# Low parts of 30 weight blocks kept in DRAM by the first group and loaded by the other three

## The chip, the cores and the metric

The kernel runs on one core of a Trainium2 chip. The metric is the device time of one execution in microseconds; the profile is one execution of the same program taken by the hardware profiler. TensorE (PE in the profile, with its weight loads as PEld) does the matmuls, VectorE is DVE, ScalarE is ACT, GpSimd is POOL, and SyncE (SP) issues most loads. Each engine works through its own queue in order.

## The reference

One layer of a hybrid block over 2048 positions of width 1024, in float32. The input is normalized and multiplied by one wide matrix `w_in`; its columns feed three branches:

```
h    = rms_norm(x, pre_mix_g)
proj = h @ w_in          # 1536 attention columns, 1792 recurrent columns, 2048 gate columns
y_a  = chunk_band_attention(q, k, v, rel_bias)      # chunks of 64, 8 earlier chunks
y_b  = rwkv7_time_mix(p_rwkv, ...)                  # a scan over the 2048 positions
merged = sigmoid(p_gate_a) * (y_a @ proj_a) + sigmoid(p_gate_b) * (y_b @ proj_b)
x = x + rms_norm(merged @ w_out)
x = x + rms_norm(relu(rms_norm(x) @ w_up)**2 @ w_down)
```

The recurrent branch mixes each column with that of the position before, derives decays and rates from it with two small matrices, and updates a 64 x 64 state per head.

## The kernel before, in words

The sequence is worked through in four groups of 512 positions. For each group there are three stages in turn: the recurrent stage (`phase_rwkv`), the attention stage (`phase_attention`) and the merge (`phase_merge`), which also normalizes the next group's input. After the four groups come the two matrices of the last line of the layer, which work on two halves of 1024 positions.

A matmul in float32 is done as three matmuls in a faster type: each operand is split into a high part, a rounded copy, and a low part, what the rounding left. The product is high x high, high x low and low x high. `wsplit` (L70) does this for a block of weights: SyncE loads the raw block of 128 x 1024 numbers (512 KB) into one of two `wraw` tiles (`load_raw`, L64), ScalarE casts it into one of two `whi` tiles (L81), and VectorE subtracts the cast from the raw block into one of two `wlo` tiles (L83). A tile is reused as soon as all that read it are through.

`dense(col)` (L118) is the product of one such block, 128 columns of `w_in`, with the group's normalized input `hh`, `hl`. It is 24 matmuls on one bank `psd`: an octet with `whi` and `hh`, an octet with `whi` and `hl`, and last an octet with `wlo` and `hh` (in the profile `hh,wlo`; the names after the arrow are sorted). So the low part is needed in the last third of a block. A recurrent stage has 30 such blocks: 14 of the recurrent columns, by `mix` (L393), and 16 of the gates, by `gate` (L786). The attention stage has 12 more. The weights are the same in every group, and each group loads and splits them anew. In the first group the first two blocks are loaded ahead, and their low parts are made by GpSimd.

`mix` takes the bank out with ScalarE into `pr` and into `out`; GpSimd copies the last column of the group before (`carry`, L399 and L400) in front of `pr`, and VectorE adds the two (L402). `rwkv_pre` and `rwkv_trans` prepare matrices for each chunk of 64 positions with many small matmuls and VectorE operations (`n2t`, `AR`, `BK`, `TQ`), `rwkv_inverse` runs 31 steps of two VectorE operations (L621, L627), and `rwkv_chunk` (L738 to L743) goes through the chunks one after the other: two matmuls on TensorE, then `ST` on VectorE, which the next chunk needs. `rwkv_post` normalizes the result; its `yn` (L761) waits for a root that GpSimd takes (L759).

The order of each engine's queue is set by a planner: it simulates the whole program with a cost for every instruction and appends to each queue whatever is ready first, earlier program text first among those that are ready. A transfer's place in SyncE's queue is planned in the same way. A few places are fixed by hand: `queue_behind` puts one instruction behind another in its queue without a wait, `follow` (L112) does so for the cast and the subtraction of a block, behind the instructions that emptied the bank three blocks before, and `place` with the numbers at the head of the file (`BLOCKS`, `TURNED`, `FIFTH`, `BONUS`, `SCORES`, `TURNS`) puts the first matmuls of the small chains behind a given matmul of the blocks of the stage, counted from its start.

Of the kernel before, what the change touches and what calls it, by code (L numbers as in the profile page):

```python
# [9 lines left out]
F32 = mybir.dt.float32  # L10
BF16 = mybir.dt.bfloat16
F32R = mybir.dt.float32r
# [4 lines left out]
DRAM = bass.MemoryType.DRAM  # L17

P = 128
D = 1024  # L20
KB = D // P
# [17 lines left out]
BONUS = {(0, 1): 138, (1, 0): 258}  # L39
SCORES = 150  # L40
TURNS = {1: (588, 592)}
DEC = math.exp(-0.5)

ATT0 = 0
# [12 lines left out]
class Block:  # L57
# [54 lines left out]
    def follow(self):  # L112

        for ins, done in zip((self.high.ins, self.low), self.emptied[-3] if len(self.emptied) > 2 else ()):
            if done is not None:
                self.queue_behind(ins, done.ins)

    def dense(self, col):  # L118

        first = bool(self.raws)  # L120
        wh, wl = self.wsplit(self.w_in(col), "w", KB, P, lower=self.nc.gpsimd if first else None)
        if first:
            n = 1 - len(self.raws)
            self.queue_behind(self.high.ins, self.highs[n])
        self.follow()
        ps = self.pd.tile([P, G], F32, tag="d", name="psd")
        terms = [(wh[:, k], wl[:, k], self.h[0][:, k], self.h[1][:, k]) for k in range(KB)]
        if first:
            pairs = [(u, h) for u, _, h, _ in terms] + [(v, h) for _, v, h, _ in terms] + [(u, l) for u, _, _, l in terms]
            self.mm = [  # L130
                self.nc.tensor.matmul(ps, l, r, start=n == 0, stop=n == len(pairs) - 1).ins
                for n, (l, r) in enumerate(pairs)
            ]
            self.queue_behind(self.mm[0], self.last_transpose)
        else:
            self.mm = self.mm3(ps, terms, True)
        self.dl += self.mm
        return ps
# [19 lines left out]
    def constants(self, ctx, mixing):  # L158
        tc, nc, a = self.tc, self.nc, self.a
        keep = ctx.enter_context(tc.tile_pool(name="const", bufs=1))  # L160
        cp = mixing.enter_context(tc.tile_pool(name="mconst", bufs=1, side="right"))
        dp = ctx.enter_context(tc.tile_pool(name="scratch", bufs=1, space=DRAM))
        nrow = sum(n for _, n in ROWS)
        self.cst = cp.tile([P, nrow], F32, name="cst")
        nc.sync.dma_start(self.cst, a["cst"])
# [279 lines left out]
    def rwkv_pre(self, g, p, rp, NA, between=lambda: None):  # L445
# [20 lines left out]
        between()  # L466
        nc.vector.tensor_scalar(tw, tw, -0.5 * DEC, -0.5 * DEC, ALU.mult, ALU.add)
        cum = tw
# [279 lines left out]
    def rwkv_post(self, p, R):  # L748
# [18 lines left out]
        for h in range(2):  # L767
            ps = self.pr.tile([C, 4, P], F32, tag="wus", name="ps_yt")
            for j in range(4):
                mm = nc.tensor.transpose(ps[:, j], yn[:, h * 4 + j], self.ident)  # L770
                if j == 0 and p in TURNS:
                    self.place(mm, TURNS[p][h])
            cs = slice(h * 4, h * 4 + 4)
# [876 lines left out]
```

## Time and profile before

| | us |
|---|---|
| median of 3 runs (lowest, highest) | 3199.82 (3198.31, 3202.85) |
| the profiled execution | 3198.07 |
| its span, first to last instruction | 3196.4 |
| TensorE busy in the span | 3147.3 |
| VectorE busy in the span | 2235.8 |
| ScalarE busy | 1578.7 |
| GpSimd busy | 613.8 |

Where the groups begin and end in the span:

| group | recurrent stage | attention stage and merge |
|---|---|---|
| 0 | 14.2 to 282.2 | 282.2 to 482.8 |
| 1 | 482.8 to 746.0 | 746.0 to 976.0 |
| 2 | 976.0 to 1239.0 | 1239.0 to 1468.6 |
| 3 | 1468.6 to 1731.6 | 1731.6 to about 1990 |

How to read the rows: a group of instructions is given by its line in the kernel, its engine, its operation and the tiles it writes and reads (out<-in), with its shape and count; then come its busy time, the mean duration of one in ns, the engine's idle time just before these instructions and what ended it. A row of a stretch of time gives the busy time and the number of instructions of each engine, the granted clock of TensorE, the busy share of the DMA rings and GB/s. Matmuls of a run overlap: eight in a row, each of 389 ns, take 1.98 us. A row of waits names the waiting instruction, whom it waited for, and the sum, the number and the longest of the waits. A row that starts with two numbers has the start in us from the begin of the span and the duration.

### The profile page before, as it was taken

The page shows a single profiled execution, that of the slowest core. Times are in us where ns is not written, and L with a number is a line of the kernel's source. Part 1 is how long each engine was busy: PE and PEld are TensorE (multiplying, and loading weights), DVE is VectorE, ACT ScalarE, POOL GpSimd, SP SyncE. Part 2 cuts the span into 40 slices and gives each one's busy share as a digit, 9 for nine tenths or more (in the row PEclk, how much of TensorE's full clock was granted, in tenths as well). Part 3 has the DMA queues.
Part 4 walks back from the last instruction along what each step waited for, and adds up shares of the span by engine and source line. Part 5 has one row for each costly group of instructions (what it writes and reads, how often), then busy time and mean ns, then how long its engine had stood idle before and what let it go on. Part 6 is the DMA issues. An engine that isn't in the chain of part 4 may idle for free. (4 is left out here: it accounts for less than half of the span.)

```text
span 3196.4 us, 49803 instructions
## 1 busy us (share of the span) xinstructions
PE 3147.3 (98%) x18800; PEld 2575.3 (81%) x18800; DVE 2235.8 (70%) x3668; ACT 1578.7 (49%) x2511; POOL 613.8 (19%) x1119
## 2 busy tenths in 40 slices
PE   8999999999999999999999999999999999999998
PEld 6877788778888877888877888888888878888887
DVE  6785667776767786767876776877656768765564
ACT  5435645445745445745534755454544454444343
POOL 3222012132112222112222101221211112210000
PEclk9999999999999999999999999999999999999999
DMA  6245473157573246574236466554877866547565
GB/s 192 86 135 189 134 259 129 60 172 244 175 260 129 77 141 245 186 235 160 94 116 228 160 208 261 192 179 162 293 268 251 281 225 213 170 156 244 191 221 174
DMA packets 197477, 598.82 MB, mean 187 GB/s; under 512 B 25570, under 2 KB 25708, under 8 KB 197236
## 3 DMA queue, kind: packets, MB, share of 16 engines
q1 hardware_dynamic: 139124, 415.24, 40.1%
q0 software_dynamic: 48896, 163.61, 13.6%
q10 hardware_dynamic: 9216, 16.78, 1.4%
q8 instruction: 148, 2.42, 0.3%
q14 instruction: 93, 0.76, 0.1%
HBM read 431.67 MB, written 167.01 MB: 187 GB/s over the span
## 5 line engine op out<-in xcount | busy, mean ns | idle before, releaser
L1469 PE MATMUL ps_dn<-fop 128*128 128x512 f32 x2688 | 610.8, 389 | 0.0
L1469 PEld LDWEIGHTS ps_dn<-fop 128*128 128x128 f32 x2688 | 504.1, 188 | 104.7 <-DVE fop L83 0.2
L81 ACT CAST whi<-wraw 128x1024 fp32r<-128x1024 f32 x232 | 243.5, 1049 | 284.4 <-PE psd L92 202.5
L83 DVE TENSOR_TENSOR wlo<-wraw,whi 128x1024 fp32r<-128x1024 f32 x230 | 280.6, 1220 | 125.4 <-ACT whi L81 80.2
L92 PE MATMUL psd<-hh,whi 128*128 128x512 f32 x1328 | 357.9, 398 | 1.1 <-ACT k L401 1.0
L92 PE MATMUL psd<-hh,wlo 128*128 128x512 f32 x1328 | 356.8, 398 | 0.0
L92 PE MATMUL psd<-hl,whi 128*128 128x512 f32 x1328 | 354.3, 397 | 0.0
L92 PEld LDWEIGHTS psd<-hl,whi 128*128 128x128 f32 x1328 | 243.6, 188 | 47.9
L92 PEld LDWEIGHTS psd<-hh,wlo 128*128 128x128 f32 x1328 | 242.7, 188 | 48.3
L92 PEld LDWEIGHTS psd<-hh,whi 128*128 128x128 f32 x1328 | 241.2, 188 | 50.0 <-ACT k L401 1.6
L83 DVE TENSOR_TENSOR fop<-xraw,fop 128x1024 fp32r<-128x1024 f32 x112 | 137.0, 1223 | 176.2 <-ACT fop L81 175.8
L81 ACT CAST fop<-xraw 128x1024 fp32r<-128x1024 f32 x112 | 117.8, 1052 | 251.0 <-PE ps_dn L1469 191.9
L1339 POOL DMA_DIRECT2D xd<-X x192 | 104.1, 542 | 380.3 <-ACT X L1336 318.2
L83 DVE TENSOR_TENSOR fop<-wdraw,fop 128x1024 fp32r<-128x1024 f32 x112 | 136.6, 1219 | 19.7 <-ACT fop L81 19.4
L81 ACT CAST fop<-wdraw 128x1024 fp32r<-128x1024 f32 x112 | 117.6, 1050 | 35.7 <-DMA wdraw<-in_w_down_dram 22.7
L994 DVE CUSTOM_DVE_ANT_0 sc<-bias,ps_s 128x640 f32<-128x640 f32 (+4 forms) x128 | 93.8, 733 | 39.3 <-PE ps_s L988 23.3
L1012 DVE TENSOR_TENSOR PTl<-ps_pt,PTh 128x640 fp32r<-128x640 f32 (+4 forms) x128 | 94.3, 737 | 27.7 <-ACT PTh L1011 26.8
L1001 ACT ACTIVATE sc<-sc,mn 128x640 f32<-128x640 f32 (+4 forms) x128 | 97.8, 764 | 31.8 <-DVE mn L994 30.4
L81 ACT CAST s12h<-s 128x1024 fp32r<-128x1024 f32 x32 | 33.7, 1053 | 155.5 <-PE ps_u L92 155.5
L92 PE MATMUL ps_p<-yh,whi 128*128 128x512 f32 x256 | 101.7, 400 | 4.9 <-DVE th L1149 2.2
L92 PE MATMUL ps_p<-yl,whi 128*128 128x512 f32 x256 | 101.5, 397 | 0.3 <-DVE yl L83 0.2
L1178 PE MATMUL ps_o<-whi,mh 128*128 128x512 f32 x256 | 100.5, 392 | 0.7 <-DVE o L1189 0.6
(374 smaller groups left out, 6804.0 us busy)
## 6 DMA issues: line engine op xcount, KB each, us to landing
wraw<-in_w_in_dram SPq DMA_DIRECT2D x168, 512.0 KB, 3.7
xraw<-xd SPq DMA_DIRECT2D x112, 512.0 KB, 4.5
xd<-X POOLq DMA_DIRECT2D x192, 256.0 KB, 4.7
wraw<-in_w_up_dram SPq DMA_DIRECT2D x80, 512.0 KB, 4.4
wdraw<-wd SPq DMA_DIRECT2D x64, 512.0 KB, 4.8
wdraw<-in_w_down_dram SPq DMA_DIRECT2D x48, 512.0 KB, 5.0
gd<-gate ACTq DMA_DIRECT2D x64, 256.0 KB, 2.5
wd<-cmb POOLq DMA_DIRECT2D x64, 256.0 KB, 3.7
```

Of the source, the lines that this page charges most:

```text
L81: high = self.high = self.nc.scalar.copy(hi, src)
L83: self.low = lower.tensor_tensor(lo, src, hi.bitcast(F32), ALU.subtract).ins
L92: mm.append(nc.tensor.matmul(ps, l, r, start=n == 0, stop=n == last).ins)
L994: least = nc.vector.tensor_tensor_reduce(sc[:, 0:n], bias[:, s0:640], pss[:, c0 : c0 + n], 1.0, 3.0e38, ALU.add, ALU.min, mn,)
L1001: nc.scalar.activation(sc[:, 0:n], sc[:, 0:n], AF.Exp, scale=-1.0, bias=mn, accum_out=sm[:, col : col + 1])
L1012: nc.vector.tensor_tensor(lv, pst[:, 0:nk], hv.bitcast(F32), ALU.subtract)
L1178: nc.tensor.matmul(ps[t], l[:, k, ts], r[:, k % 2], start=k == 0 and j == 0, stop=k == KB - 1 and j == 2)
L1339: nc.gpsimd.dma_start(self.xd[q][i // 2][:, i % 2], src)
L1469: nc.tensor.matmul(ps, o[:, l, k, sl], o[:, r, k], start=start and n == 0, stop=stop and n == end)
```

## The change

`LOWS` names the blocks 12 to 41 of `w_in` by their number, which are the 14 recurrent blocks and the 16 gate blocks. When a group comes to such a block for the first time, it splits it as before and GpSimd then issues a store of the low part into a DRAM tile of its own. When a later group comes to it, the raw block is loaded and cast as before, and SyncE issues a load of the kept low part into the `wlo` tile; VectorE's subtraction is gone there. `follow` passes over the low part that it no longer has. The 12 attention blocks stay as they were.

```diff
 TURNS = {1: (588, 592)}
+LOWS = range(12, 42)
...
         for ins, done in zip((self.high.ins, self.low), self.emptied[-3] if len(self.emptied) > 2 else ()):
-            if done is not None:
+            if done is not None and ins is not None:
                 self.queue_behind(ins, done.ins)
 
     def dense(self, col):
 
         first = bool(self.raws)
-        wh, wl = self.wsplit(self.w_in(col), "w", KB, P, lower=self.nc.gpsimd if first else None)
+        kept = self.lows.get(col)
+        if kept is None:
+            wh, wl = self.wsplit(self.w_in(col), "w", KB, P, lower=self.nc.gpsimd if first else None)
+            if col in self.keep_lows:
+                kept = self.lows[col] = self.dp.tile([P, KB, P], F32, name=f"wlow{col // P}")
+                self.nc.gpsimd.dma_start(kept, wl.bitcast(F32))
+        else:
+            raw = self.load_raw(self.w_in(col), KB, P)
+            wh, wl = (self.wp.tile([P, KB, P], F32R, tag="w" + x, bufs=2, name="w" + n) for x, n in (("h", "hi"), ("l", "lo")))
+            self.high = self.nc.scalar.copy(wh, raw)
+            self.low = None
+            self.nc.sync.dma_start(wl.bitcast(F32), kept)
         if first:
...
-        dp = ctx.enter_context(tc.tile_pool(name="scratch", bufs=1, space=DRAM))
+        dp = self.dp = ctx.enter_context(tc.tile_pool(name="scratch", bufs=1, space=DRAM))
+        self.lows = {}
+        self.keep_lows = {i * P for i in LOWS}
```

## The prediction, made before the changed kernel ran

> **What bounds the kernel now.** I read the page's busy line first, then its groups, then each recurrent stage with the busy times by stage, then who ended TensorE's waits there, and last the order of time around the longest wait.
>
> ```profile
> span 3196.4 us, 49803 instructions
> ```
> ```profile
> PE 3147.3 (98%) x18800; PEld 2575.3 (81%) x18800; DVE 2235.8 (70%) x3668; ACT 1578.7 (49%) x2511; POOL 613.8 (19%) x1119
> ```
> ```profile
> L1469 PE MATMUL ps_dn<-fop 128*128 128x512 f32 x2688 | 610.8, 389 | 0.0
> ```
> ```profile
> L83 DVE TENSOR_TENSOR wlo<-wraw,whi 128x1024 fp32r<-128x1024 f32 x230 | 280.6, 1220 | 125.4 <-ACT whi L81 80.2
> ```
>
> TensorE is busy 98% of the span. The last row is the work that the change takes away in part: VectorE's subtraction for one 512 KB weight block, 1.22 us, 230 times. The four rows below are the recurrent stages of groups 0 to 3, each from the first `psd` matmul to the first of the attention.
>
> ```profile
> core 0: us, PE busy (x) PEld busy (x) DVE busy (x) ACT busy (x) POOL busy (x), PEclk, DMA share, GB/s
> 14.20:282.20 268.00, 263.73 (x2188) 210.92 (x2189) 201.40 (x413) 122.93 (x208) 72.29 (x117) 1.00 0.44 141
> 482.80:746.00 263.20, 259.79 (x2190) 209.26 (x2189) 193.49 (x399) 118.83 (x203) 71.58 (x124) 1.00 0.41 132
> 976.00:1239.00 263.00, 259.79 (x2190) 209.24 (x2189) 193.50 (x399) 118.82 (x203) 71.65 (x124) 1.00 0.40 132
> 1468.60:1731.60 263.00, 259.80 (x2190) 209.24 (x2189) 193.51 (x399) 118.83 (x203) 71.65 (x124) 1.00 0.40 132
> ```
>
> In the stages that lose the subtractions TensorE idles 3.4, 3.2 and 3.2 us, 9.8 us together. VectorE is busy 193.5 of 263 us there (74%), so it is loaded but not the bound. The clock is 1.00 throughout. Who ended TensorE's waits in the third of these stages:
>
> ```profile
> engine line waited for: us in total, times, longest us
> PE ps_st L738 <- DVE ST L743: 1.1, 1, 1.1
> PE ps_s L723 <- DVE TQ L716: 0.4, 1, 0.4
> PE ps_g L92 <- DVE yn L761: 0.4, 1, 0.4
> PE psd L92 <- ACT k L401: 0.3, 1, 0.3
> ```
>
> None of them is for a low part. VectorE ends 1.9 us of waiting in a stage, and 1.1 of it is one step of the recurrence.
>
> **The change part by part.**
>
> *Subtractions removed, groups 1 to 3.* 90 x 1.22 = 110 us of VectorE's time go, 36.6 us in a stage. What that is worth is what it does to the three waits on VectorE. For the 1.1 us one, VectorE in order of time:
>
> ```profile
> 1134.35 1.22 DVE L83 TENSOR_TENSOR wlo<-wraw,whi 128x1024 fp32r<-128x1024 f32 x1
> ```
> ```profile
> 1136.53 0.73 DVE L514 SCALAR_TENSOR_TENSOR AR<-k,nkk,E 64x512 f32<-64x512 f32 x1
> 1137.84 0.17 DVE L489 TENSOR_SCALAR n2t<-ps_ss 128x8 f32<-128x8 f32 x1 [0.58 <-PE ps_ss L487]
> 1138.04 0.75 DVE L514 SCALAR_TENSOR_TENSOR AR<-k,nkk,E 64x512 f32<-64x512 f32 x1
> ```
> ```profile
> 1145.05 0.75 DVE L533 SCALAR_TENSOR_TENSOR r<-r,cst,tk 128x512 f32<-128x512 f32 x1
> 1145.71 0.47 DVE L743 SCALAR_TENSOR_TENSOR ST<-ps_st,gC,S 128x64 f32<-128x64 f32 x2
> ```
>
> From 1137.84 VectorE works without a break until the awaited `ST`. The subtraction at 1134.35 lies ahead of the `n2t` operation, which waits for TensorE anyway; with the order kept, taking 1.22 us away only lengthens that 0.58 us wait, and the gain is 0. If the planner uses the room to put the second `AR` (0.75 us) ahead of `n2t`, the `ST` comes 0.75 us sooner, and somewhat more if another one moves up. I take 0.8 us: the planner places by readiness, and all the inputs of `AR` are there. The other two waits:
>
> ```profile
> 1204.07 0.69 DVE L1231 TENSOR_TENSOR cmb<-cmb 128x512 f32<-128x512 f32 x1 [7.58 <-DMA cmb<-in_w_down_dram]
> ```
> ```profile
> 1237.38 0.69 DVE L761 TENSOR_TENSOR yn<-ps_y,grs 128x512 f32<-128x512 f32 x1 [2.07 <-POOL grs L759]
> ```
>
> Ahead of `TQ` VectorE had idled 7.58 us for a DMA, and ahead of `yn` it idled 2.07 us for GpSimd. A lighter VectorE does nothing for either: 0. Sum 3 x 0.8 = -2.4 us; bounds 0 and all the idle time, -9.8 us. What is late next in these places is the same `TQ`, `yn` and the PSUM release by `k`.
>
> *Low parts loaded, groups 1 to 3.* 90 loads of 512 KB are added on SP's queue. A load's tile is free when TensorE has used the low part of the block before the last, and TensorE uses the low part in the last third of a block. So the room is from the end of one `hh,wlo` octet to the start of the next but one. At a stage's start, with the DMA rings full in between, and at the tightest place:
>
> ```profile
> 979.58 1.98 PE L92 MATMUL psd<-hh,wlo 128*128 128x512 f32 x8
> ```
> ```profile
> 990.97 1.98 PE L92 MATMUL psd<-hh,wlo 128*128 128x512 f32 x8
> ```
> ```profile
> 1159.68 1.98 PE L92 MATMUL psd<-hh,wlo 128*128 128x512 f32 x8
> ```
> ```profile
> 1170.56 1.98 PE L92 MATMUL psd<-hh,wlo 128*128 128x512 f32 x8
> ```
> ```profile
> 980.00:985.00 5.00, 5.00 (x23) 4.13 (x22) 2.01 (x3) 3.28 (x6) 1.90 (x6) 1.00 1.01 337
> ```
>
> Room 990.97 - 981.56 = 9.4 us and 1170.56 - 1161.66 = 8.9 us. The same-sized weight loads of the stage, by their line:
>
> ```profile
> L67 SPq DMA_DIRECT2D wraw<-in_w_in_dram x30: 327/328/333, 979.1 to 1234.8; - x30
> ```
> ```profile
> DMA to landing us min/median/max: 3.4/3.7/7.6
> ```
>
> Issue 0.33 and landing 3.7: 4.0 us in the median, 7.9 at worst, against 8.9: hidden. In the full window a further 0.52 MB at 337 GB/s adds 1.6 us: 9.5 against 9.4, so 0.1 us at one place in a stage; I take 0. The stage's DMA share rises from 0.40: the 30 raw loads are 15.7 of its 34.7 MB (132 GB/s x 263 us), so 30 more make about 0.40 x 50.4/34.7 = 0.58, below full. On SP's queue a raw load can now stand behind a low load that waits for TensorE. The raw load stood behind VectorE's subtraction before, since that read the raw tile last; now ScalarE's cast alone frees it. Behind a low load it starts at latest at the end of block n-2 and lands 4 to 8 us later, with two blocks (six octets, 1170.56 - 1159.68 = 10.9 us, 1.81 us each) until its block begins: hidden. Attention's `KK` and `VV` loads follow the last low load in the same way.
>
> *Low parts stored, group 0.* 30 DMAs on GpSimd's queue, each after the subtraction. The nearest rows are the 512 KB store of `kc` and the carry copies that could queue behind a store (in the stage 14.2 to 282.2):
>
> ```profile
> L960 POOL DMA_DIRECT2D kc<-KK x12: 682/724/736, 297.9 to 1355.2; - x12
> ```
> ```profile
> DMA to landing us min/median/max: 3.1/3.8/6.7
> ```
> ```profile
> L399 POOL COPY pr<-carry 128x1 f32<-128x1 f32 x13 | 9.5, 729 | 32.1 <-DVE k L402 15.5 <-DVE r L402 9.1 <-DVE X L627 3.5
> ```
> ```profile
> L400 POOL COPY carry<-pr 128x1 f32<-128x1 f32 x14 | 5.3, 379 | 35.4 <-ACT pr L398 35.3
> ```
>
> 30 x 0.72 = 21.7 us on an engine that is busy 72.3 of 268 us. GpSimd idles 67.5 us ahead of those copies alone, so most stores lie in idle time; a store caught in front of a copy costs at most 0.72 us, passed on to VectorE's `out` and the release of `pr`. Bounds 0 and +21.7; I take +0.5, near the end at which GpSimd's idle time lies. The store also holds the low tile until it has landed: 0.72 + 3.8 = 4.5 us (7.4 at worst) after a subtraction. The closest pair of subtractions into one tile is
>
> ```profile
> 100.78 1.18 DVE L83 TENSOR_TENSOR wlo<-wraw,whi 128x1024 fp32r<-128x1024 f32 x1
> ```
> ```profile
> 108.40 1.22 DVE L83 TENSOR_TENSOR wlo<-wraw,whi 128x1024 fp32r<-128x1024 f32 x1
> ```
>
> 6.4 us apart: hidden in the median, 1.0 us late at worst.
>
> *TensorE's order.* The planner orders each engine by simulated costs, so a new order follows from other costs. In the trace it shows as broken runs: an undisturbed matmul of this shape takes 389 ns, the `psd` ones more on average in the third stage:
>
> ```profile
> L92 PE MATMUL psd<-hh,wlo 128*128 128x512 f32 x240 | 63.9, 397 | 0.0
> ```
>
> (397 - 389) x 720 = 5.8 us in a stage is what the breaks cost. Half as many or half again as many make 2.9 us a stage, 8.6 over three, either way; nothing says which: 0.
>
> *Sum.* The profiled execution took 3198.07 us for a span of 3196.4. 3198.07 - 2.4 + 0.5 = 3196.2. The median of the runs shown is 3199.82, 1.75 above the profiled one, so in its terms 3197.9.
>
> [...]
>
> **The rivals.**
>
> *A, faster.* VectorE's release carries further: the chains reach TensorE earlier, all idle time goes from three stages, 3199.8 - 9.8 = 3190.0; with half of the breaks gone as well, 3181. For: VectorE at 74% and in-order. Against: only 1.9 of some 3.2 us wait for VectorE, and 0.8 of that for other causes. Chance 0.19; the weight-load rule above adds 0.01.
>
> *B, slower: the low load lands late.* It decides where issue and landing exceed 8.9 us. If a low load must let a raw load of 3.7 us pass first in a full window, it lands after 0.33 + 7.6 + 3.7 = 11.6 us: 2.2 us late at the 9.4 us room, 2.7 at 8.9. With four such places in a stage (three at its start, one at 1160) 4 x 2.3 x 3 = +28: 3227. Against: median landing 3.7, rings at 0.40. Chance 0.08.
>
> *C, slower: a worse order.* Half again as many breaks in three stages: 3199.8 + 8.6 = 3208.4. For: the places of the chains in TensorE's order are numbers written for the old costs. Against: those numbers bind the costliest chains either way. Chance 0.12.
>
> *D, slower: GpSimd's stores.* Every store stands in front of a copy that VectorE waits for: +21.7, 3221.5. The idle time above speaks against it: 0.02. [...]
>
> **How the numbers follow.** A difference under 0.2% (6.4 us) can't be told from none here. My forecast and all small sums lie inside it: 0.58. Faster by more is A, 0.20; slower by more is B, C and D, 0.22. The likeliest time is 3197.9. The range reaches from 3189, past A's idle time, to 3209, past C; left out are A with the breaks (0.07), B and D.
>
> **What would show it.** Right: 140 `wlo<-wraw` subtractions instead of 230, VectorE near 157 us in stages 1 to 3, TensorE's busy time there unchanged at 259.8 and its idle time at 2.4 to 3.2 us; no wait of TensorE for a low load; a DMA share near 0.58. Wrong: TensorE waiting for `wlo` (B), a `psd` mean well off 397 ns (A or C), more than 4.3 us of idle in stage 0 or VectorE waiting for a carry copy (D).

## The result, and the profile after

| | before | after |
|---|---|---|
| median (lowest, highest) of 4 runs each, us | 3199.07 (3196.69, 3202.85) | 3216.47 (3210.49, 3219.30) |
| ratio, 95% interval | | 1.0051 (1.0033 to 1.0068) |
| profiled execution, its span, us | 3198.07, 3196.4 | 3219.30, 3217.3 |

The change makes the kernel slower, by 17.4 us in the median. The profiled execution of the changed kernel is the slowest of its four. Line numbers of the changed kernel are 1 to 14 higher: the cast in a group that loads its low parts is L131, the copies of the inverse XT (L637 before) and Z (L655) are L651 and L669, a gate's emptying of its bank (L790) is L804.

The page's head, and the groups of the subtraction and of the new loads (KB each, median us to landing):

```profile
span 3217.3 us, 49953 instructions
...
PE 3155.4 (98%) x18800; PEld 2581.4 (80%) x18800; DVE 2136.9 (66%) x3578; ACT 1578.3 (49%) x2511; POOL 606.9 (19%) x1149
...
L84 DVE TENSOR_TENSOR wlo<-wraw,whi 128x1024 fp32r<-128x1024 f32 x140 | 170.9, 1221 | 90.3 <-ACT whi L82 60.9
...
wlo<-wlow SPq DMA_DIRECT2D x90, 512.0 KB, 4.6
```

The 90 subtractions are gone and VectorE is 99 us lighter. TensorE issues the same 18800 matmuls, is busy 8.1 us longer (3155.4 against 3147.3) and idle 12.8 us longer (61.9 against 49.1). The four recurrent stages, each from its first `psd` matmul to the first of the attention:

```profile
core 0: us, PE busy (x) PEld busy (x) DVE busy (x) ACT busy (x) POOL busy (x), PEclk, DMA share, GB/s
14.00:284.90 270.90, 265.69 (x2188) 212.88 (x2189) 201.74 (x413) 122.69 (x208) 89.68 (x147) 0.99 0.60 197
486.30:753.50 267.20, 261.77 (x2189) 210.26 (x2188) 161.63 (x370) 119.11 (x203) 63.69 (x124) 0.99 0.54 184
983.40:1253.50 270.10, 262.00 (x2190) 210.50 (x2189) 161.67 (x370) 119.06 (x203) 63.64 (x124) 0.99 0.55 183
1482.10:1751.00 268.90, 261.97 (x2189) 210.43 (x2189) 161.73 (x370) 119.25 (x203) 63.67 (x124) 0.99 0.55 184
```

Their lengths are up by 2.9, 4.0, 7.1 and 5.9 us, 19.9 of the 20.9 us by which the span grew. All the rest of the kernel is 1.0 us longer. Who ended TensorE's waits in the third of these stages (line waited for: total, times, longest):

```profile
PE ps_t L674 <- ACT Z L669: 2.7, 2, 2.3
PE psd L93 <- ACT gate L804: 2.0, 1, 2.0
PE ps_y L756 <- DVE ST L757: 1.1, 1, 1.1
PE ps_g L93 <- DVE yn L775: 0.9, 1, 0.9
PE ps_A L599 <- DVE BR L583: 0.5, 1, 0.5
```

No wait is for a low part. The two longest are new, and both are for ScalarE, an engine that the change leaves with the same work. Its queue in order of time, before and then after, around the end of the second inverse of that stage:

```profile
1179.43 1.06 ACT L81 CAST whi<-wraw 128x1024 fp32r<-128x1024 f32 x1
...
1181.54 0.69 ACT L790 ACTIVATE gate<-psd,hgb 128x512 f32<-128x512 f32 x1
...
1184.87 1.06 ACT L81 CAST whi<-wraw 128x1024 fp32r<-128x1024 f32 x1 [2.64 <-PE psd L92]
1190.42 1.24 ACT L637 COPY XT<-XD 32x512 f32<-32x512 f32 x2 [4.49 <-DVE XD L632]
```

```profile
1192.83 1.25 ACT L651 COPY XT<-XD 32x512 f32<-32x512 f32 x2 [5.20 <-DVE XD L646]
...
1195.25 1.04 ACT L131 CAST whi<-wraw 128x1024 fp32r<-128x1024 f32 x1
1196.20 0.68 ACT L804 ACTIVATE gate<-psd,hgb 128x512 f32<-128x512 f32 x1
...
1206.03 1.04 ACT L131 CAST whi<-wraw 128x1024 fp32r<-128x1024 f32 x1 [6.78 <-DMA wraw<-in_w_in_dram]
1207.10 1.18 ACT L669 COPY Z<-ps_t 32x512 f32<-32x512 f32 x2
```

Counting the stage's blocks from 0: before, the cast of block 26 (1179.43) and the emptying of block 24's bank (1181.54) stood ahead of XT, and so did the cast of block 27 (1184.87); ScalarE then waited 4.49 us for VectorE's XD with nothing urgent behind. After, XT stands ahead of all three. ScalarE waits 5.20 us for the same XD, and the cast (1195.25) and the emptying (1196.20) wait behind it; TensorE needs that bank for block 26 and stands for 2.0 us. In the third and fourth stage a second wait follows: the late cast frees its raw tile late, the next raw loads are issued at 1196.32 and 1198.69 and land 9.6 and 10.2 us later, the cast at 1206.03 waits for one of them, and Z waits behind that cast. The likely reason that the planner wrote this order is that its simulation with a lighter VectorE ended the inverse sooner: in the trace XT starts 209.4 us into the stage instead of 214.4. What the simulation held is not shown; that the old order returns when VectorE keeps its subtractions is shown below.

The 8.1 us of added busy time lie mostly at four places. Each row is 3.4 us with the clock in the column behind GpSimd's:

```profile
250.30:253.70 3.40, 3.40 (x60) 3.28 (x56) 2.13 (x4) 0.00 (x0) 0.38 (x1) 0.51 0.20 77
700.90:704.30 3.40, 3.40 (x10) 2.63 (x9) 0.00 (x0) 0.96 (x2) 3.18 (x6) 0.50 0.92 280
1209.50:1212.90 3.40, 3.40 (x13) 2.73 (x12) 0.00 (x0) 1.88 (x4) 0.00 (x0) 0.50 0.94 332
1707.80:1711.20 3.40, 3.40 (x32) 2.67 (x31) 0.00 (x0) 1.98 (x5) 0.00 (x0) 0.50 0.99 389
```

TensorE ran at half clock for 3.41 us behind one of the waits in each stage (behind the wait for TQ of 1.8 us, the bank, Z of 2.3 us, and in the fourth stage Z of 1.1 us), 1.7 us lost each time, 6.8 in all. Before, the clock was 1.00 from 20.9 us on to the last stretch.

So the 20.9 us are: bank waits 3 x 2.0 = 6.0; Z 4.4 against 0.8, 3.6; `ps_o` 2.0 against 0.6, 1.4; `yn` 3.0 against 1.6, 1.4; `BR` 1.5, new; TQ -0.4; together 13.5, of which smaller waits give 0.7 back (12.8 idle); half clock 6.8; and 1.3 of busy time that I did not trace to a place.

### The profile page after: what moved, and what is told of

It is laid out like the page before. It is cut to its first block, busy times and chain, and to the rows that moved or that the text cites. A ratio compares the mean times of both kernels' runs of the same rounds, so it can differ in the third digit from the quotient of the medians.

```text
span 3217.3 us, 49953 instructions
## 1 busy us (share of the span) xinstructions
PE 3155.4 (98%) x18800; PEld 2581.4 (80%) x18800; DVE 2136.9 (66%) x3578; ACT 1578.3 (49%) x2511; POOL 606.9 (19%) x1149
## 5 line engine op out<-in xcount | busy, mean ns | idle before, releaser
L84 DVE TENSOR_TENSOR wlo<-wraw,whi 128x1024 fp32r<-128x1024 f32 x140 | 170.9, 1221 | 90.3 <-ACT whi L82 60.9
L131 ACT CAST whi<-wraw 128x1024 fp32r<-128x1024 f32 x90 | 94.4, 1049 | 130.5 <-PE psd L93 110.7
L727 DVE TENSOR_TENSOR TQ<-ps_tq,id 128x256 f32<-128x256 f32 x32 | 13.5, 423 | 154.6 <-PE ps_tq L724 154.6
```

What stands on the lines that cost most here:

```text
L84: self.low = lower.tensor_tensor(lo, src, hi.bitcast(F32), ALU.subtract).ins
L131: self.high = self.nc.scalar.copy(wh, raw)
L727: nc.vector.tensor_tensor(TQ[:, cs, 0], ps[:, :, 0], self.id64[:, None, :].to_broadcast((P, 4, C)), ALU.add)
```

## The experiments

Two theories. **Order**: the loss is ScalarE's queue, in which XT moved ahead, with the half clock behind its waits. **Traffic**: the loss is the 30 stores and 90 loads. Ratios are to the kernel before on the same chip, whose median is 3199.01 us for the first four experiments and 3198.75 for the next four.

**The 30 stores alone.** All groups split as before.

```diff
-            if col in self.keep_lows:
-                kept = self.lows[col] = self.dp.tile([P, KB, P], F32, name=f"wlow{col // P}")
+            if col in self.keep_lows and col not in self.stored:
+                self.stored.add(col)
+                kept = self.dp.tile([P, KB, P], F32, name=f"wlow{col // P}")
...
+        self.stored = set()
```

> Only the 30 stores of the first group; the other groups split as in the kernel before, and every engine's order but GpSimd's is that of the kernel before. Theory Order (the loss comes from ScalarE's queue, where the planner put the XT copies ahead of a finished gate): nothing to lose here, 3199 within 2 us. Theory Traffic (the added DMAs make others land late, and an in-order engine passes that on): the cmb load ahead of TQ lands 0.7 to 1 us later, TensorE's wait at ps_s in stage 0 grows from 0.93 to about 1.8 us and may bring 3.4 us of half clock behind it: 3201 to 3203, all of it in stage 0.

Measured 3203.42 us, ratio 1.0011 (1.0002 to 1.0020): +4.4 in the medians, a little above what Traffic expected. The trace shows Traffic's mechanism in stage 0. The granted clock of the profiled execution is 0.998, against 0.999 before; one stretch of 3.41 us at half clock, 1.7 of 3199.7 us, would account for that. VectorE and TensorE's wait there, before and then in this run:

```profile
247.29 0.69 DVE L1231 TENSOR_TENSOR cmb<-cmb 128x512 f32<-128x512 f32 x1 [8.33 <-DMA cmb<-in_w_down_dram]
...
PE ps_s L723 <- DVE TQ L716: 0.9, 1, 0.9
```

```profile
247.99 0.69 DVE L1247 TENSOR_TENSOR cmb<-cmb 128x512 f32<-128x512 f32 x1 [9.14 <-DMA cmb<-in_w_down_dram]
...
PE ps_s L739 <- DVE TQ L732: 1.8, 1, 1.8
```

Two stores lie on the rings beside that `cmb` load, which lands 8.0 us after its issue instead of 7.3; its subtraction stands ahead of TQ in VectorE's queue, and the recurrence waits for TQ.

**Stores, loads, and the subtractions kept.** VectorE still subtracts, into the raw tile, which nobody reads.

```diff
-            self.low = None
+            self.low = self.nc.vector.tensor_tensor(raw, raw, wh.bitcast(F32), ALU.subtract).ins
```

> Stores and 90 low loads as in the change, but VectorE keeps its subtraction in groups 1 to 3 (into the raw tile, where nobody reads it), so VectorE is as loaded as before. Theory Order: the planner sees the inverse end as late as before, the XT copies stay behind the gate, no 2.0 us waits: 3200 to 3204. Theory Traffic: the loads are all there, so 3213 to 3217 as with the change.

Measured 3201.86, ratio 1.0005 (0.9997 to 1.0014). All the traffic is there and most of the loss is not; in the third stage XT again follows the cast of block 26 and the emptying of block 24's bank:

```profile
1183.52 1.05 ACT L131 CAST whi<-wraw 128x1024 fp32r<-128x1024 f32 x1
...
1185.62 0.69 ACT L804 ACTIVATE gate<-psd,hgb 128x512 f32<-128x512 f32 x1
...
1193.61 1.25 ACT L651 COPY XT<-XD 32x512 f32<-32x512 f32 x2 [3.57 <-DVE XD L646]
```

The loads add nothing over the stores alone (-1.6 us, within the uncertainty).

**The order without the loads.** The changed kernel with one low part loaded in a stage instead of 30; it leaves out the right low parts of the other blocks.

```diff
-            wh, wl = (self.wp.tile([P, KB, P], F32R, tag="w" + x, bufs=2, name="w" + n) for x, n in (("h", "hi"), ("l", "lo")))
+            wh = self.wp.tile([P, KB, P], F32R, tag="wh", bufs=2, name="whi")
...
-            self.nc.sync.dma_start(wl.bitcast(F32), kept)
+            if len(self.dl) == 0:
+                self.one_low = self.wp.tile([P, KB, P], F32R, tag="wl", bufs=2, name="wlo")
+                self.nc.sync.dma_start(self.one_low.bitcast(F32), kept)
+            wl = self.one_low
```

> As the change, with the orders of TensorE, ScalarE and VectorE unchanged from it, but only one low part is loaded in each of stages 1 to 3 and used for all 30 blocks: 3 loads instead of 90 (the low products are then those of the first block). Theory Order: the 2.0 us wait of psd for a gate stays in all three stages, only the wait for Z behind the late raw load shrinks: 3209 to 3214. Theory Traffic: 3202 to 3204, the stores' loss alone.

Measured 3215.30, ratio 1.0050 (1.0037 to 1.0062): all of the loss with 3 loads instead of 90, and 1.3 us more than Order expected at most. TensorE, VectorE, ScalarE and GpSimd have the same orders as in the changed kernel's trace. TensorE's waits over the whole span:

```profile
PE psd L93 <- ACT gate L807: 5.9, 3, 2.0
...
PE ps_t L677 <- ACT Z L672: 3.1, 4, 2.1
```

The bank wait is there three times; the long one for Z only once. Traffic falls as the main cause.

**The order put back.** The changed kernel, with the two XT copies of the second inverse queued behind the cast of block 26 and the emptying of block 24's bank in stages 1 to 3. Only ScalarE's order differs. (`casts` and `turned`, in this run and the next, list the casts and the XT copies of the stage; the lines that fill them are left out.)

```diff
...
+            if g:
+                for ins in self.turned[2:]:
+                    self.queue_behind(ins, self.emptied[done + 24][0].ins)
+                    self.queue_behind(ins, self.casts[26])
```

> As the change, but in stages 1 to 3 the two XT copies of the second inverse stand behind the cast of block 26 and the emptying of block 24 in ScalarE's queue; nothing else moves. Theory Order: the 2.0 us waits go, the raw loads behind the casts start 9 us earlier so the waits for Z (2.3 and 1.1 us) go too, and with both the half clock: 3 x (2.0 + 1.1 + 1.7) = 14 us less than the change, 3201 to 3205. Theory Traffic: the loads are all there; only the 2.0 us go at most, 3209 to 3214.

Measured 3204.24, ratio 1.0019 (1.0010 to 1.0028). Stages 1 to 3 and the waits of the third:

```profile
484.60:747.80 263.20, 259.79 (x2192) 209.08 (x2190) 161.86 (x370) 118.50 (x201) 63.19 (x123) 1.00 0.55 188
978.00:1241.20 263.20, 259.79 (x2192) 209.11 (x2191) 161.87 (x370) 118.44 (x201) 63.00 (x123) 1.00 0.56 189
1470.00:1733.40 263.40, 259.78 (x2190) 209.03 (x2189) 161.86 (x370) 118.86 (x201) 63.45 (x124) 1.00 0.56 188
...
PE ps_y L757 <- DVE ST L758: 1.1, 1, 1.1
PE ps_g L93 <- DVE yn L776: 0.9, 1, 0.9
```

The stages are back at the 263 us of before, bank and Z waits and the half clock are gone, with the low loads and their share of the rings (0.55 to 0.56) still there. Order's part is 3216.47 - 3204.24 = 12.2 us in the medians; the two ratios lie 0.0032 (10 us) apart, and their intervals do not meet. The profiled execution, 3200.77 us, is one of the shortest of the eleven: the four with a granted clock of 0.999 took 3200.6 to 3203.0 us, the four with 0.997 took 3206.7 to 3208.8. So in others the clock was lower somewhere, where no trace shows.

**The other way round: the kernel before with XT put ahead.** Nothing is stored or loaded.

```diff
...
+            if g:
+                for ins in (self.casts[26], self.emptied[done + 24][0].ins):
+                    self.queue_behind(ins, self.turned[-1])
```

> The kernel before, no low part stored or loaded; in stages 1 to 3 ScalarE's two copies of the second inverse (XT, L638) are only put ahead of the cast of block 26 and the emptying of the bank of block 24. Theory Order (the loss lies in ScalarE's queue): TensorE waits for the emptied bank, then for Z, in three stages; since the inverse ends here some 5 us later in its stage than in the changed kernel, the wait at the bank is longer, 2 to 7 us, with half clock behind most of them: 3199 plus 3 times 4 to 9, 3211 to 3226, and a granted clock near 0.5 for 3.4 us after the waits. Rival Traffic (the loss lies in the transfers, the order only goes with them): without transfers the order costs its idle time of some 2 us a stage at most and no clock: 3199 to 3205.

Measured 3221.71, ratio 1.0069 (1.0057 to 1.0082): +23.0. ScalarE and TensorE's longest wait in the third stage:

```profile
1196.77 1.24 ACT L638 COPY XT<-XD 32x512 f32<-32x512 f32 x2 [8.60 <-DVE XD L633]
1198.04 0.69 ACT L791 ACTIVATE gate<-psd,hgb 128x512 f32<-128x512 f32 x1
1198.63 1.03 ACT L81 CAST whi<-wraw 128x1024 fp32r<-128x1024 f32 x1
...
PE psd L92 <- ACT whi L81: 5.6, 1, 5.6
```

Two copies placed otherwise in three stages cost at least about as much as the whole change: 23.0 us against 17.4 in the medians, with intervals that meet. That it is more fits the later end of the inverse with the subtractions still in VectorE's queue: XT starts 213.5 us into the stage, not 209.4. Expected was the wait at the bank; it ended at the cast behind it, in the same queue. The clock was at half for 6.83 us in each of the three stages, not 3.4 (granted clock 0.996 over the profiled execution); part of that lies in the wait itself. Behind ScalarE's order a few others shift: one subtraction a stage goes behind a `yf` operation, and `ps_s` and `ps_y` of one place alternate differently.

**The relief alone.** The changed kernel with the order put back, one store and three loads; the low parts are again left out.

> The changed kernel with the copies put back behind the cast and the emptying, one store and three loads instead of 30 and 90: it leaves out the right low parts in groups 1 to 3 (one low part serves all blocks of a stage). So the removed subtractions stand alone. Prediction's first term: 3199 - 2.4 = 3196.6, from 3189 to 3199. Theory Order with the relief worth nothing: 3198 to 3201. If the stores cost what the run with stores alone says (4 us), it stands 3 to 5 us under the changed kernel with the copies put back (3204.2). If it stays at 3203 or more, the loss that is left isn't the stores' but that of the new order on VectorE and TensorE.

Measured 3199.23, ratio 1.0000 (0.9991 to 1.0009). The third stage, its two longest waits, and VectorE around the recurrence step for which the prediction had expected a gain:

```profile
976.00:1238.70 262.70, 259.81 (x2190) 209.12 (x2189) 161.93 (x370) 119.25 (x203) 63.88 (x124) 1.00 0.40 130
...
PE ps_y L762 <- DVE ST L763: 1.1, 1, 1.1
PE ps_g L93 <- DVE yn L781: 0.8, 1, 0.8
...
1134.98 1.50 DVE L534 SCALAR_TENSOR_TENSOR AR<-k,nkk,E 64x512 f32<-64x512 f32 x2
1137.58 0.17 DVE L509 TENSOR_SCALAR n2t<-ps_ss 128x8 f32<-128x8 f32 x1 [1.10 <-PE ps_ss L507]
...
1144.61 0.46 DVE L763 SCALAR_TENSOR_TENSOR ST<-ps_st,gC,S 128x64 f32<-128x64 f32 x2
```

VectorE loses 31.6 us in the stage, and the stage is 0.3 us shorter. The wait for TQ (0.4) is gone, and the one for `yn` has grown from 0.4 to 0.8. Both `AR` operations now stand ahead of `n2t`, and `ST` starts at 1144.61 instead of 1145.71, in a stage that starts at 976.0 in both. TensorE waits 1.1 us for it all the same, because its matmul that needs `ST` has also moved: 493 `psd` matmuls of the stage lie ahead of it instead of 497, and four of them are 0.9 us.

This kernel stands 5.0 us under the one with the order put back, with the same orders of TensorE, VectorE and ScalarE; that is the price of the transfers in the medians. (With the subtractions kept, the same transfers cost 2.9 us, -1.0 to 4.5 by the interval.) The two profiled executions, both at 1.00 in all four stages, are 3.5 us apart: stage 0 is 267.7 us here and 269.4 there, and the next three 262.7 here and 263.2, 263.2 and 263.4 there.

**The combination's subtraction behind TQ**, in the changed kernel with the order put back.

```diff
...
+            if 3 in self.tq:
+                self.queue_behind(op.ins, self.tq[3])
```

> The changed kernel with the copies put back, and also the combination's first subtraction, which waits for a DMA, queued behind the last TQ on VectorE. Theory Landing (in stage 0 the stores make a load land later, and VectorE's queue passes that on to TensorE): the wait of 2.1 us at the stage's ps_s goes to under 0.5, and no half clock follows: 1.6 to 3.5 us under 3204.2, 3200.7 to 3202.6. Rival (TQ itself or GpSimd's stores late): the wait stays, 3204.

Measured 3201.62, ratio 1.0009 (1.0000 to 1.0018): 2.6 us less, though the intervals of the two overlap. The wait of 2.1 us in stage 0 is gone, the only stage where the edit changes VectorE's order; now the longest for VectorE there is

```profile
PE ps_g L93 <- DVE yn L776: 1.2, 1, 1.2
```

The profiled execution is one of the longer ones, 3205.05 us: it has 10.24 us of half clock in the next stage, 5.1 us lost (granted clock 0.997, where the relief alone had 0.999).

**The same edit in the kernel before.**

> The kernel before with the same edit alone: in all four stages the combination's subtractions that wait for a DMA are queued behind the last TQ. Theory Landing: the waits of ps_s, 0.93 in stage 0 and 0.4 in three, go: 3199 - 2.1 = 3196.9. Rival: what is late next (the weight of the chunk, the bank) takes their place: 3199.

Measured 3200.45, ratio 1.0002 (0.9993 to 1.0011). The rival holds: the waits for TQ are gone in all four stages, and in the third the one for `yn` rose from the 0.4 us of before to

```profile
PE ps_g L92 <- DVE yn L761: 1.2, 1, 1.2
```

None of these versions beats the kernel before: the relief is worth nothing that can be measured, and the rest of the change costs.

**The price of a wait by itself.**

```python
for n in (64, 256, 512, 768, 896, 1024, 1152, 1280, 1536, 2048):   # columns to add
    for i in range(14):
        ...                            # ps: a new bank
        nc.tensor.matmul(ps[:, 0:C], y[:, 0:P], m[:, 0:C], start=True, stop=True)      # waits for VectorE
        for k in range(48 + 3 * (i % 7)):
            nc.tensor.matmul(ps, y[:, 0:P], y[:, 0:G], start=True, stop=True)
        ...                            # m: additions on VectorE of n columns, from ps
```

> Nothing of the layer is computed here, so its time has nothing to do with the others'. 140 runs of 48 to 66 matmuls of 128 x 512 (11 to 15 us), and after each run TensorE waits for one to four additions on VectorE and then goes on: ten lengths of the wait, from some 0.5 to some 3.3 us, 14 times each, at changing distances. Theory Clock (a wait of about 2 us costs more than itself, because half clock follows it, by chance of where it falls): no half clock behind the waits under about 1.5 us, behind a part of those from 1.6 to 2.5 us, behind nearly all above 3 us; each time 3.4 us long, so that some 15 matmuls start at 454 ns apart instead of 227. Rival (the half clock in the changed kernel belongs to what else runs there, the small matmuls of the inverse and the transfers): full clock behind all waits up to 3 us.

The granted clock over the run is 0.977. The trace, grouped by the length of the wait:

```
wait, us             0.32  0.52  0.78  1.33  1.47  1.60  1.92  2.06  2.32  3.05
half clock behind it    0     0     0     0     0     0     6     4     5    11
of                     14    14    14    14    14    14    14    14    14    13
```

The rival falls as it was put: nothing else runs here, and half clock followed 6 of the 14 waits of 1.92 us. In the changed kernel it followed less idle time as well (last section). The 3.42 us around a wait of 1.93 us, the 3.41 us after it, and a stretch of the same grid that holds 1.01 of another 1.93 us:

```profile
1219.79:1223.21 3.42, 1.49 (x7) 0.97 (x7) 1.68 (x3) 0.00 (x0) 0.00 (x0) 1.00 0.00 0
1223.21:1226.62 3.41, 3.41 (x9) 2.64 (x9) 0.00 (x0) 0.00 (x0) 0.00 (x0) 0.50 0.02 5
1236.86:1240.27 3.41, 2.40 (x11) 2.04 (x12) 0.83 (x2) 0.00 (x0) 0.00 (x0) 1.00 0.01 2
```

All half-clock stretches of this run begin on one grid of 3.4133 us (to 0.001 us); those of the changed kernel's trace, at 250.341, 700.900, 1209.486 and 1707.832 us, are 132, 149 and 146 times 3.4133 us apart. In this run a stretch of the grid with 1.91 us or more of idle time was followed by one at half clock each time, 26 of 26; with 1.88 us or less, never. A wait of 2 us that lay across a grid line so that neither side held that much had none behind it: 8 of the 14 of 1.92 us here, and in the changed kernel the third stage's bank wait of 2.04 us, with 0.9 us on one side and 1.1 us on the other.

## Why the prediction was wrong, step by step

*TensorE's order* is the step that failed. It said that a new order "shows as broken runs" of the `psd` matmuls and took 0, with 8.6 us either way. The order that changed is ScalarE's. The two XT copies, which wait for VectorE, were put ahead of a cast and an emptying that TensorE waits for. That is worth 12.2 us of the 17.4 (the order put back), and 23.0 in the kernel before. The rows that could have told it were in the trace: ScalarE idle 4.49 us before XT, waiting for XD, with the casts at 1179.43 and 1184.87 and the emptying at 1181.54 ahead. The step costed the breaks in TensorE's queue, and not the queue that links VectorE to TensorE.

*Rival C* had the sign, but by another mechanism and with less than half the size, and its sign in the profile would have denied it: the `psd` mean that I named is unchanged (those of the other two `psd` groups of the stage went from 397 and 396 to 399 and 400),

```profile
L93 PE MATMUL psd<-hh,wlo 128*128 128x512 f32 x240 | 63.2, 397 | 0.0
```

*Clock*: the prediction noted 1.00 throughout and took a wait for its own length. Four waits, of 1.1 to 2.3 us, had 3.41 us at a clock of 0.50 behind them, 1.7 us lost each, 6.8 us that no term held. In the run of waits alone 26 of the 55 waits from 1.92 us on had half clock behind them, and none of the 84 up to 1.60 us; in the changed kernel 1.25 us of idle time within one stretch was enough once.

*Low parts stored*: +0.5 was too small; the stores alone measured +4.4 (0.6 to 6.4 by the ratio's interval). The sign for rival D came, 5.2 us of idle time in stage 0 against 4.3, but not its mechanism: an issue took 0.53 to 0.78 us, the longer wait is for TQ, and among VectorE's longest waits in stage 0 none is for a copy of `carry`. The step counted the issues and the tile, and not that a load which VectorE's queue is waiting for lands later with 512 KB stores on the rings beside it (8.0 us instead of 7.3). The wait for the same load in the third stage, 7.58 us, stood in the prediction, used only to say that a lighter VectorE would not help; it also says that TQ is late whenever that load is.

*Low parts loaded*: 0 holds for the low parts themselves (no wait for one; 3 loads instead of 90 change nothing that can be measured). They landed in 4.6 us in the median and 11.5 at worst, with a ring share of 0.54 to 0.55 against the forecast 0.58. The worst landing is past the 8.9 us of room, as rival B had it, but none was waited for, and B fell. One sentence was wrong: that "ScalarE's cast alone frees" the raw tile was taken for a relief, without asking what that cast stands behind.

*Subtractions removed*: 140 left, VectorE at 161.7 us against "near 157", and worth 0.0 (-2.9 to +2.9 by the interval) instead of -2.4. VectorE lost less than 36.6 us a stage because the records of neighbouring instructions overlap (the one at 1145.05 lasts 0.75 us, the next starts at 1145.71), so a subtraction's 1.22 us are not all its own. In the trace three stages gained 0.5 + 0.3 + 0.3 us. The mechanism named did come, `AR` ahead of `n2t` and `ST` 1.1 us sooner, but it gained nothing there: the prediction had kept TensorE's order, and the planner moved the matmul that waits for `ST` forward as well, so the wait is still 1.1 us. That TQ's wait could not shrink was wrong in stages 1 to 3, and made no difference, since `yn` took its place, as "what is late next" had it. No run shows the weight loads' share as a source of gain, for which rival A has 0.01 of its chance: with the relief alone that share is 209.12 of 262.70 us in the third stage, where before it was 209.24 of 263, and the time is the same (ratio 1.0000).

Not settled: the 5.0 us that the transfers cost. In the profiled executions 3.5 us of it are 1.7 in stage 0 and 0.5, 0.5 and 0.7 in the next three. The rest of the difference of the medians fits the lower granted clock of some executions of the kernel with the order put back (0.997 against 0.999), but no trace shows where that lies.

## What to carry to other kernels

When a planner writes the queues, making one engine lighter moves instructions in all queues. Look on each of the others for an instruction that waits for the lightened engine, and ask what stands behind it in that queue; moving two such copies past one cast and one emptying in each of three stages cost some 12 us here, where 90 subtractions less (99 us) on an engine that was not the bound gained nothing that can be measured. When a late operation comes sooner, look also at whether the instruction that waits for it has moved. Price a new wait of TensorE by its length, and look in the trace for half clock behind it: in the changed kernel it stood behind waits of 1.1, 1.8, 2.0 and 2.3 us and cost 1.7 us each time.

## What the runs showed of the hardware that was not expected

In the run with matmuls of 128x512 and waits alone (granted clock 0.977), 1.91 us idle within one stretch of the grid of 3.4133 us was followed by half clock in the whole next one, 1.88 us was not. In three cases, where a wait of 3.05 us reached 0.8 to 1.05 us into the half-clock stretch, the next stretch was at half clock too (6.83 us).

In the changed kernel's own trace less idle time was enough. The stretches ahead of its four half-clock ones, and then one behind which the clock stayed at 1.00:

```profile
246.93:250.34 3.41, 1.62 (x30) 1.34 (x32) 1.86 (x5) 0.00 (x0) 0.54 (x1) 1.00 0.54 215
697.49:700.90 3.41, 1.41 (x7) 0.89 (x6) 1.38 (x2) 2.92 (x5) 1.46 (x3) 1.00 0.61 171
1206.07:1209.49 3.42, 1.40 (x65) 1.25 (x65) 0.00 (x0) 2.84 (x4) 0.00 (x0) 1.00 1.01 400
1704.42:1707.83 3.41, 2.16 (x70) 1.97 (x71) 0.00 (x0) 2.75 (x6) 0.00 (x0) 1.00 1.02 415
1694.18:1697.59 3.41, 1.90 (x8) 1.59 (x9) 1.21 (x2) 2.96 (x4) 2.71 (x6) 1.00 0.74 177
```

TensorE is idle for 1.78, 2.00, 2.01 and 1.25 us in the first four and for 1.51 us in the last. The two with the least idle time of the four hold 30 and 70 matmuls, most of them small ones of the chains; the one that had no half clock behind it holds 8 of 128x512. Whether the size of the matmuls has a part in it is not shown: no run tried it by itself.
